# A modulation stream moved off TensorE's row products: VectorE, ScalarE and GpSimd accumulate, two-column products sum

## The chip, the cores and the metric

The kernel runs on one core of one Trainium2 chip. The metric is the device time of one execution in microseconds. A core has TensorE (PE; its weight loads are shown as PEld), VectorE (DVE), ScalarE (ACT) and GpSimd (POOL), each with a queue that it works off in order, and a queue (SP) that issues the transfers from device memory.

## The reference, cut to what matters

Two sequences, of 256 and 512 tokens, go through two layers of width 1024. In each layer a vector `c` of the sequence gives six modulation vectors, which scale and shift the normed input of the mixer and of the feed-forward network and gate their outputs:

```python
def trunk(x, c, adaln_w, adaln_b, norm_g, ...):
    for l in range(DEPTH):
        mod = jax.nn.silu(c) @ adaln_w[l] + adaln_b[l]
        sh1, sc1, g1, sh2, sc2, g2 = [t[:, None, :] for t in jnp.split(mod, 6, axis=-1)]
        h = rmsnorm(x, norm_g[l, 0]) * (1 + sc1) + sh1
        y = mlstm_mixer(...) if l % N_MIXERS == 0 else swa_mixer(...)
        x = x + g1 * y
        h = rmsnorm(x, norm_g[l, 1]) * (1 + sc2) + sh2
        x = x + g2 * conv_ffn(...)
    return rmsnorm(x, final_g)
```

`adaln_w[l]` is 1024 x 6144 float32: 24 MB in each layer, read once, for two vectors only. The product is small in arithmetic and large in bytes. The first mixer is an mLSTM with four heads, run forwards and backwards; the second is windowed attention.

## The kernel before, in words

All 768 tokens of both sequences are worked on together. Activations lie transposed, 128 channels on the partitions and tokens along the free axis. Products that need float32 accuracy are made of three products: each operand is split into a rounded part and a remainder (`fp_copy_split`: ScalarE writes the rounded `whi`, L236; VectorE subtracts it from the source to get `wlo`, L237), and TensorE adds high x high, high x low and low x high (L230 is the line of its helper `mm`).

Weights and modulation rows come through one set of staging buffers, `raw`, of five slots of 128x1024 (L245 issues the transfer). SP issues them in order; an issue that waits for a free slot holds up all those behind it.

The modulation is worked off beside the first mixer. `adaln_w[l]` is cut into six groups of 1024 columns, and each group into eight rows of 128x1024 (a "row" below is one such 128x1024 block). Groups 0 and 1 of layer 0 are needed at once and are done in the opening (`vector`); the change does not touch them. The rest was done in two streams, written as generators, of which the mixer takes a step at fixed places in its own code:

- `fillp`: groups 2 to 5 of layer 0 (`adaln_g`). For each row TensorE makes four products with `silc` (silu(c), two used columns in 32) as the stationary operand, one in each quarter of its columns, and accumulates over eight rows in one PSUM bank `ps`. At the end of a group the sums, which lie along the free axis, are copied to `sb` (a tile in a `raw` slot; VectorE and ScalarE, half each) and turned into columns by two transposes.
- `fill`: all six groups of layer 1 (`adaln_v`). For each row VectorE makes two operations, one for each sequence: `acc[:, s] = row * silc[:, k, s] + acc[:, s]` (L472; for the first row of a group a plain scaling, L470). The accumulator `ada` has one buffer. At the end of a group TensorE sums over the partitions by four products with 32 columns of ones, `sb` takes the result, and four transposes make columns.

In both, VectorE then adds the bias and writes `mod[l]`, and for groups 1 and 4 the `gain`.

Steps are taken: in the heads' query and key projections (`gemmT`, after each evacuation, and once after each half), in the value projection (`gemmN`, `values`, on every second token tile from `fill`, on the others from `fillp`), twice ahead of each sequence in a head's second part, and after each of the 16 products of the output gate. Counted from the code, the mixer offers 50 steps to `fill`, which has 49 to give, and 37 to `fillp`, which has 36.

Other work that the prediction's steps touch: the scores' weights are built by ScalarE as `E` and split into `PT`; each head's output `hs` is divided by `dn`, its mean square `ss` goes through a power on GpSimd (L942), and TensorE transposes it (L949). GpSimd also adds the masks `kct` (L829) and multiplies the gate `sg` (L966). The norms sum squares over partitions by products with `inv`, a 128x2 moving operand, the squares being the stationary one.

The order on each engine is written by a planner that plays the program through with its own costs, except in the opening, where TensorE, ScalarE and VectorE follow the order of the code.

Of the kernel before, what the change touches and what calls it, by code (L numbers as in the profile page):

```python
# [46 lines left out]
NG = 0  # L47
AB = NG + 32
# [97 lines left out]
class Net:  # L146
# [260 lines left out]
                )  # L407
        yield

    def adaln_g(self, l, grp):  # L410

        nc = self.nc
        fetch = lambda k: self.raw(
            self.io["adaln_w"][l, k * P : (k + 1) * P, grp * 1024 : (grp + 1) * 1024]
        )
        part = fetch(0)
        yield
        ps = self.ps()
        for k in range(KC):
            cur = part  # L420
            if k < KC - 1:
                part = fetch(k + 1)
            for g in range(4):
                r0 = 32 * g
                self.mm(
                    ps[r0 : r0 + 32, :256], self.silc[:, k, :], cur[:, g * 256 : (g + 1) * 256], k == 0, k == KC - 1
                )
            if k < KC - 1:
                yield
        sb = self.stg.tile([P, 2, P], F32, tag="raw", name=self.nm("sb"), bufs=5)  # L430
        nc.vector.tensor_copy(sb[:, 0], ps[:, :P])
        nc.scalar.copy(sb[:, 1], ps[:, P : 2 * P])
        pt = self.ps()[:, : 2 * P]
        for b in range(2):
            nc.tensor.transpose(pt[:, b * P : (b + 1) * P], sb[:, b], self.ident)
        src = pt.rearrange("p (b g s) -> p g b s", b=2, g=4)
        dst = self.mod[l][:, grp * 8 : (grp + 1) * 8, :].rearrange("p (g b) s -> p g b s", g=4)
        ab = self.cst(AB + 48 * l + 8 * grp, 8).rearrange("p (g b) -> p g b", g=4)
        for s in range(2):
            nc.vector.tensor_tensor(dst[:, :, :, s], src[:, :, :, s], ab, ALU.add)  # L440
        i = {1: 0, 4: 1}.get(grp)
        if i is not None:
            for s in range(2):
                nc.vector.scalar_tensor_tensor(
                    self.gain[l][i][:, :, s], self.mod[l][:, grp * 8 : (grp + 1) * 8, s], 1.0,
                    self.cst(NG + (2 * l + i) * 8, 8), ALU.add, ALU.mult,
                )
        yield

    def adaln_v(self, l, pool):  # L450

        nc = self.nc
        stt = nc.vector.scalar_tensor_tensor
        rows = [(grp, k) for grp in range(6) for k in range(KC)]
        fetch = lambda grp, k: self.raw(
            self.io["adaln_w"][l, k * P : (k + 1) * P, grp * 1024 : (grp + 1) * 1024]
        )
        raw = fetch(*rows[0])
        yield
        for grp, k in rows:  # L460
# [3 lines left out]
            if (grp, k) != rows[-1]:  # L464
                raw = fetch(*rows[grp * KC + k + 1])
            for s in range(2):
                w = self.silc[:, k, s : s + 1]
                if k == 0:
                    with self.tc.issue_after(self.behind_gates.ins):
                        nc.vector.tensor_scalar(acc[:, s], row, w, None, ALU.mult)  # L470
                else:
                    stt(acc[:, s], row, w, acc[:, s], ALU.mult, ALU.add)  # L472
            if k < KC - 1:
                yield
                continue
            ps = self.ps()
            for s in range(2):
                for b in range(2):
                    r0 = 32 * (2 * s + b)
                    self.mm(ps[r0 : r0 + 32, :], self.ones[:, :32], acc[:, s, b * 512 : (b + 1) * 512], True, True)  # L480
            sb = self.stg.tile([P, 2, 256], F32, tag="raw", name=self.nm("sb"), bufs=5)
            sb = [sb[:, z] for z in range(2)]
            nc.vector.tensor_copy(sb[0], ps[:, :256])
            nc.scalar.copy(sb[1], ps[:, 256:])
            pt = self.ps()
            for t in range(4):
                nc.tensor.transpose(
                    pt[:, t * P : (t + 1) * P], sb[t // 2][:, (t % 2) * P : (t % 2 + 1) * P], self.ident
                )
            src = pt.rearrange("p (t g s) -> p g t s", t=4, g=4)[:, :, :, 0]  # L490
            ab = self.cst(AB + 48 * l + 8 * grp, 8).rearrange("p (b t) -> p b t", b=2)
            dst = self.mod[l][:, grp * 8 : (grp + 1) * 8, :].rearrange("p (b t) s -> p b t s", b=2)
            for s in range(2):
                nc.vector.tensor_tensor(dst[:, :, :, s], src[:, 2 * s : 2 * s + 2], ab, ALU.add)
            i = {1: 0, 4: 1}.get(grp)
            if i is not None:
                for s in range(2):
                    stt(
                        self.gain[l][i][:, :, s], self.mod[l][:, grp * 8 : (grp + 1) * 8, s], 1.0,
                        self.cst(NG + (2 * l + i) * 8, 8), ALU.add, ALU.mult,  # L500
                    )
            yield


    def modulated(self, l, i):
# [260 lines left out]
    def mlstm(self, pool, xt, rows, raws):  # L766
        nc, io = self.nc, self.io
# [6 lines left out]
        F, a, M, z = (B[0:G, j] for j in range(4))  # L774
# [12 lines left out]
        with self.tc.manual_schedule(engines={eng.PE, eng.Activation, eng.DVE}):  # L787
# [14 lines left out]
            for s0, s1 in SEQS:  # L802
                b = slice(s0, s1)
# [18 lines left out]
        for h in range(4):  # L822
# [13 lines left out]
            for i in range(2 if h else 0):  # L836
                t = self.slab([P, 2, 2, T], R)
                for c, w in self.halves(U_MIN + 3 * h + i):
                    for q in (0, 1):
                        keep(t, i, c)(q, self.gemmT(w, q))  # L840
                        if q <= c or h > 1:
                            self.step(self.fill)
                    self.step(self.fillp)
                qk.append(t)
            qt, kt = qk

            def values():
# [4 lines left out]
                def evac(t, o):  # L852
                    self.fp_copy_split(v[:, 0, t, :256], v[:, 1, t, :256], o)
                    if t % 2 == 0:
                        self.step(self.fill)
                    elif h:
                        self.step(self.fillp)

                self.gemmN(U_MIN + 3 * h + 2, evac)
                return v  # L860
# [49 lines left out]
            ss = pool.tile([P, T6], F32, tag="ss", name=self.nm("ss"), bufs=2)  # L910
            for q, (s0, s1) in enumerate(SEQS):
                n = (s1 - s0) // P
                self.step(self.fillp, 2)
                hq = []
                for i in range(n):
                    ti = s0 // P + i
# [688 lines left out]
    def first(self, pool):  # L1605
# [11 lines left out]
        def chain(*gens):  # L1617
            for g in gens:
                yield from g
# [4 lines left out]
        for _ in chain(self.fillp, self.fill):  # L1624
            pass
        return act

# [128 lines left out]
```

## Time and profile before

| | us |
|---|---|
| median of 3 runs | 1871.75 (1870.81 to 1874.26) |
| the profiled execution: its time | 1875.08 |
| its span, first to last instruction | 1873.0 |
| TensorE busy in the span | 1801.3 (96%) |
| VectorE | 1400.9 (75%) |
| ScalarE | 911.0 (49%) |
| GpSimd | 497.9 (27%) |
| granted TensorE clock, mean | 0.988 |

"Busy" is the time in which at least one instruction of the engine ran; TensorE's instructions overlap, so the distance between two starts says more of their price than their own durations. Rows of the timeline give start, duration, engine, line, operation, tile written <- tiles read, shapes and count; in brackets stands the idle time before and what ended it. Rows of one tile give shortest, median and longest duration in ns. Rows of groups give count, busy time in us, mean ns, and the idle time before them.

### The profile page before, as it was taken

How to read it: one execution, taken by the hardware profiler on the slowest of the kernel's cores; microseconds unless marked ns; L12 is line 12 of the kernel's file. 1: busy time of each engine (PE TensorE's matmuls, PEld its weight loads, DVE VectorE, ACT ScalarE, POOL GpSimd, SP SyncE). 2: the span in 40 equal slices, each digit the busy share in tenths (PEclk: the TensorE clock that was granted, in tenths of full speed). 3: DMA queues.
4: the chain of work that ended last, by engine and by line, in shares of the span. 5: the costliest groups of instructions: out<-in, count | busy, mean ns of one | idle time of the engine just before them, and what ended most of it. 6: DMA issues, size and time to landing. Idle time of an engine off the chain costs nothing. (4 is left out here: it accounts for less than half of the span.)

```text
span 1873.0 us, 29153 instructions
## 1 busy us (share of the span) xinstructions
PE 1801.3 (96%) x11306; PEld 1662.3 (89%) x11306; DVE 1400.9 (75%) x2306; ACT 911.0 (49%) x1841; POOL 497.9 (27%) x390
## 2 busy tenths in 40 slices
PE   6989999999999999999999999989999999999997
PEld 5968887878988999999999898879989999999996
DVE  4866567685689777777777768875997777777777
ACT  4544334444455444444444556763565444444443
POOL 2011001031024333333331313330134333333322
PEclk9999999999999999999999999999999999999999
DMA  8353466555212222222222221212222222222211
GB/s 325 108 165 134 152 197 205 162 167 193 97 50 74 68 68 68 68 68 68 68 68 82 101 90 41 89 55 90 79 79 79 68 68 68 68 68 68 68 35 68
DMA packets 64246, 184.49 MB, mean 99 GB/s; under 512 B 6167, under 2 KB 23831, under 8 KB 64108
## 3 DMA queue, kind: packets, MB, share of 16 engines
q1 hardware_dynamic: 64108, 182.63, 30.1%
q8 instruction: 89, 1.46, 0.3%
q14 instruction: 49, 0.40, 0.1%
HBM read 176.17 MB, written 6.43 MB: 97 GB/s over the span
## 5 line engine op out<-in xcount | busy, mean ns | idle before, releaser
L236 ACT CAST whi<-raw 128x1024 fp32r<-128x1024 f32 x237 | 249.0, 1051 | 389.9 <-PE pa L230 198.6
L237 DVE TENSOR_TENSOR wlo<-raw,whi 128x1024 fp32r<-128x1024 f32 x237 | 316.3, 1335 | 108.8 <-ACT whi L236 107.7
L230 PE MATMUL pa<-slab,whi 128*128 128x256 f32 (+1 forms) x1472 | 346.9, 333 | 6.2 <-DVE slab L719 6.2
L230 PEld LDWEIGHTS pa<-slab,whi 128*128 128x128 f32 x1472 | 253.2, 190 | 33.1 <-DVE slab L719 7.1
L719 DVE SCALAR_TENSOR_TENSOR slab<-pa,mod,slab 128x256 f32<-128x256 f32 (+1 forms) x368 | 207.5, 591 | 70.9 <-PE pa L230 70.6
L230 PE MATMUL ps<-zh,whi 128*128 128x256 f32 (+2 forms) x688 | 233.4, 340 | 6.3 <-ACT whi L236 2.6
L230 PE MATMUL pa<-slab,wlo 128*128 128x256 f32 (+1 forms) x736 | 234.9, 331 | 0.0
L230 PE MATMUL ps<-zh,wlo 128*128 128x256 f32 (+2 forms) x688 | 228.3, 334 | 3.8 <-DVE wlo L237 3.8
L230 PE MATMUL ps<-zl,whi 128*128 128x256 f32 (+2 forms) x688 | 228.7, 334 | 1.4 <-DVE zl L539 0.9
L1275 PE MATMUL ps<-zh,whi 128*128 128x384 f32 x504 | 171.0, 339 | 6.4 <-ACT ps L1330 5.4
L1276 PE MATMUL ps<-zl,whi 128*128 128x384 f32 x504 | 169.7, 337 | 0.8 <-DVE zl L1233 0.8
L1277 PE MATMUL ps<-zh,wlo 128*128 128x384 f32 x504 | 169.0, 335 | 0.0
L230 PEld LDWEIGHTS pa<-slab,wlo 128*128 128x128 f32 x736 | 139.3, 190 | 12.9 <-DVE wlo L237 0.9
L230 PEld LDWEIGHTS ps<-zh,whi 128*128 128x128 f32 x688 | 132.2, 192 | 20.3 <-issue 3.5
L230 PEld LDWEIGHTS ps<-zh,wlo 128*128 128x128 f32 x688 | 132.2, 192 | 14.6 <-DVE wlo L237 4.6
L230 PEld LDWEIGHTS ps<-zl,whi 128*128 128x128 f32 x688 | 132.3, 192 | 10.7 <-DVE zl L539 1.1
L1531 POOL TENSOR_TENSOR slab<-slab 128x772 f32<-128x772 f32 x44 | 87.4, 1987 | 190.3 <-DVE slab L1503 178.9
L1306 POOL TENSOR_TENSOR raw<-raw,raw 128x512 f32<-128x512 f32 x40 | 53.7, 1341 | 291.7 <-DVE wlo L237 243.8
L1502 DVE SCALAR_TENSOR_TENSOR slab<-slab,cstt,slab 128x771 f32<-128x771 f32 x88 | 106.2, 1208 | 25.4 <-ACT slab L1500 25.4
L1503 DVE SCALAR_TENSOR_TENSOR slab<-slab,cstt,slab 128x771 f32<-128x771 f32 x88 | 120.1, 1365 | 0.8
L1303 POOL TENSOR_TENSOR raw<-raw 128x512 f32<-128x512 f32 x40 | 64.8, 1619 | 186.1 <-DMA raw<-in_w_dram 178.4
L472 DVE SCALAR_TENSOR_TENSOR ada<-raw,silc,ada 128x1024 f32<-128x1024 f32 x84 | 111.5, 1358 | 2.6 <-DMA raw<-in_adaln_w_dram 2.6
(300 smaller groups left out, 4163.8 us busy)
## 6 DMA issues: line engine op xcount, KB each, us to landing
raw<-in_w_dram SPq DMA_DIRECT2D x208, 512.0 KB, 3.7
raw<-in_adaln_w_dram SPq DMA_DIRECT2D x84, 512.0 KB, 4.5
slab<-in_x_dram SPq DMA_DIRECT2D x12, 512.0 KB, 7.7
slab<-in_adaln_w_dram SPq DMA_DIRECT2D x12, 512.0 KB, 10.3
slab<-mrows SPq DMA_DIRECT2D x8, 384.0 KB, 6.0
xs<-slab SPq DMA_DIRECT2D x6, 512.0 KB, 2.9
bt<-brow SPq DMA_DIRECT2D x16, 192.0 KB, 3.2
slab<-xs SPq DMA_DIRECT2D x6, 512.0 KB, 5.7
```

Source lines behind the costliest of these rows:

```text
L230: self.last_mm = self.nc.tensor.matmul(out, lhsT, rhs, start=start, stop=stop)
L236: nc.scalar.copy(hi, src)
L237: return nc.vector.tensor_tensor(lo, src, hi.bitcast(F32), ALU.subtract)
L472: stt(acc[:, s], row, w, acc[:, s], ALU.mult, ALU.add)
L719: self.nc.vector.scalar_tensor_tensor(x, o, self.mod[l][:, gc + c, q : q + 1], x, ALU.mult, ALU.add)
L1275: mm(o, wh[:, k], hi[k], start=start and k == 0, stop=False, skip_group_check=True)
L1276: mm(o, wh[:, k], lo[k], start=False, stop=False, skip_group_check=True)
L1277: mm(o, wl[:, k], hi[k], start=False, stop=k == 3, skip_group_check=True)
L1303: tt(q[2], q[2], q[3], ALU.add)
L1502: stt(y[:, 1:], u[:, :-1], w(0), y[:, 1:], ALU.mult, ALU.add)
L1503: stt(y[:, :-1], u[:, 1:], w(2), y[:, :-1], ALU.mult, ALU.add)
L1531: nc.gpsimd.tensor_tensor(y, y, yrow[:, j], ALU.mult)
```

## The change

The two streams become one, `later`: layer 0's groups 2 to 5, then all of layer 1's, 80 rows in order. A row's first sequence is still accumulated by one operation of VectorE. For the second, ScalarE scales the row in place, and GpSimd adds it to the accumulator. For the first row of a group ScalarE writes the accumulator directly. At the end of a group each 128x128 block of the accumulator is the stationary operand of a product with two columns of ones, 16 products in all, which leave the sums as columns in PSUM; `sb` and the transposes are gone. All the places that took a step of `fillp` take one of `fill`; 87 steps are offered, and 81 are to be given.

```diff
-    def adaln_g(self, l, grp):
...
-    def adaln_v(self, l, pool):
+    def later(self, pool):
         nc = self.nc
+        rows = [(l, grp, k) for l, grps in ((0, range(2, 6)), (1, range(6))) for grp in grps for k in range(KC)]
...
+        for n, (l, grp, k) in enumerate(rows):
             if k == 0:
                 acc = pool.tile([P, 2, 1024], F32, tag="ada", name=self.nm("ada"), bufs=1)
             row = raw
+            if n + 1 < len(rows):
+                raw = fetch(*rows[n + 1])
+            with self.tc.issue_after(self.behind_gates.ins) if n == 0 else ExitStack():
+                self.rows_in(acc, row, k)
             if k < KC - 1:
                 yield
                 continue
-            ps = self.ps()
+            pm = self.ps()[:, : 4 * KC]
             for s in range(2):
-                for b in range(2):
-                    r0 = 32 * (2 * s + b)
-                    self.mm(ps[r0 : r0 + 32, :], self.ones[:, :32], acc[:, s, b * 512 : (b + 1) * 512], True, True)
...
+                for b in range(KC):
+                    i = 2 * (s * KC + b)
+                    self.mm(pm[:, i : i + 2], acc[:, s, b * P : (b + 1) * P], self.ones[:, 0:2], True, True)
+            src = pm.rearrange("p (s b z) -> p s b z", s=2, z=2)
...
+    def rows_in(self, acc, row, k):
+        nc = self.nc
+        w = [self.silc[:, k, s : s + 1] for s in range(2)]
+        if k == 0:
+            nc.vector.tensor_scalar(acc[:, 0], row, w[0], None, ALU.mult)
+            nc.scalar.activation(acc[:, 1], row, AF.Copy, scale=w[1])
+            return
+        nc.vector.scalar_tensor_tensor(acc[:, 0], row, w[0], acc[:, 0], ALU.mult, ALU.add)
+        nc.scalar.activation(row, row, AF.Copy, scale=w[1])
+        nc.gpsimd.tensor_tensor(acc[:, 1], acc[:, 1], row, ALU.add)
...
-                    self.step(self.fillp)
+                    self.step(self.fill)
...
-        self.fillp = chain(*(self.adaln_g(0, grp) for grp in range(2, 6)))
-        self.fill = self.adaln_v(1, pool)
+        self.fill = self.later(pool)
```

More of the change, by code (lines that the diff above doesn't have):

```diff
@@ L408, in vector @@
         yield
-    def adaln_g(self, l, grp):
+    def later(self, pool):
         nc = self.nc
[L413 to L417, printed above, removed]
-        ps = self.ps()
[L419 to L433, printed above, removed]
-        for b in range(2):
[L435 to L448, printed above, removed]
-    def adaln_v(self, l, pool):
[L452 to L455, printed above, removed]
+        rows = [(l, grp, k) for l, grps in ((0, range(2, 6)), (1, range(6))) for grp in grps for k in range(KC)]
+        fetch = lambda l, grp, k: self.raw(
             self.io["adaln_w"][l, k * P : (k + 1) * P, grp * 1024 : (grp + 1) * 1024]
@@ L475, in adaln_v @@
                 continue
-            ps = self.ps()
+            pm = self.ps()[:, : 4 * KC]
             for s in range(2):
-                for b in range(2):
-                    r0 = 32 * (2 * s + b)
-                    self.mm(ps[r0 : r0 + 32, :], self.ones[:, :32], acc[:, s, b * 512 : (b + 1) * 512], True, True)
[L481 to L492, printed above, removed]
+                for b in range(KC):
+                    i = 2 * (s * KC + b)
+                    self.mm(pm[:, i : i + 2], acc[:, s, b * P : (b + 1) * P], self.ones[:, 0:2], True, True)
+            src = pm.rearrange("p (s b z) -> p s b z", s=2, z=2)
+            ab = self.cst(AB + 48 * l + 8 * grp, 8)
             for s in range(2):
-                nc.vector.tensor_tensor(dst[:, :, :, s], src[:, 2 * s : 2 * s + 2], ab, ALU.add)
+                dst = self.mod[l][:, grp * 8 : (grp + 1) * 8, s]
+                nc.vector.tensor_tensor(dst, src[:, s, :, 0], ab, ALU.add)
             i = {1: 0, 4: 1}.get(grp)
@@ L912, in mlstm @@
                 n = (s1 - s0) // P
-                self.step(self.fillp, 2)
+                self.step(self.fill, 2)
                 hq = []
```

19 lines of the change are left out of this document (3 added, 16 removed).

## The prediction

> **What bounds the kernel now.** I read the page first, then the stretch of the first mixer in windows, then what TensorE waits for there, then single rows for prices.
>
> The page: TensorE is busy nearly throughout, VectorE three quarters of the time, GpSimd little.
>
> ```profile
> span 1873.0 us, 29153 instructions
> PE 1801.3 (96%) x11306; PEld 1662.3 (89%) x11306; DVE 1400.9 (75%) x2306; ACT 911.0 (49%) x1841; POOL 497.9 (27%) x390
> ```
>
> The change touches only the stretch from 85 to 446 us, where the modulation rows are worked in. In windows (length, busy time of each engine, granted clock, DMA), with the waits of TensorE in that stretch (total, times, longest):
>
> ```profile
> 85.00:365.00 280.00, 267.54 (x1902) 228.53 (x1901) 184.14 (x333) 114.16 (x310) 21.85 (x14) 0.99 0.52 168
> 365.00:446.00 81.00, 77.00 (x438) 65.33 (x438) 63.57 (x78) 31.26 (x64) 22.96 (x18) 0.96 0.51 163
> ...
> PE pa L949 <- ACT hs L945: 5.8, 2, 5.4
> PE ps L230 <- DVE wlo L237: 3.8, 4, 1.7
> PE ps L230 <- ACT whi L236: 2.6, 2, 1.4
> PE pa L230 <- ACT hs L936: 1.5, 1, 1.5
> PE ps L487 <- ACT sb L484: 0.9, 1, 0.9
> PE ps L487 <- DVE sb L483: 0.6, 1, 0.6
> ```
>
> TensorE works 344.5 of 361 us, so the stretch is TensorE's work plus some 16 us of waits. VectorE is at 247.7 us (69%), ScalarE at 145.4, GpSimd at 44.8. The change pays only through TensorE work or those waits; a saved VectorE microsecond alone is worth nothing.
>
> **TensorE work removed.** Layer 0's groups 2 to 5 lose 32 row products (four 32-column products each, eight records), layer 1 loses 24 products with ones, and both lose 24+8 transposes. Busy time of each in the stretch (TensorE first), and two places that show start-to-start prices:
>
> ```profile
> 85.00:446.00 361.00, 19.54 (x256) 6.94 (x256) 120.41 (x96) 0.00 (x0) 0.98 0.52 167
> 85.00:446.00 361.00, 7.43 (x48) 1.07 (x48) 0.00 (x0) 0.00 (x0) 0.98 0.52 167
> ...
> 293.77 0.66 PE L487 MATMUL ps<-kct,sb 128*128 128x128 f32 x4 [0.95 <-ACT sb L484]
> 294.26 0.38 PE L949 MATMUL pa<-kct,hs 128*128 128x128 f32 x2
> ```
>
> Row products 19.5 us (first row, tile silc), ones products 7.4 (second, tile ones). Four transposes last 294.26−293.77 = 0.49 us, so 32 are 3.9. Together 30.9 us. The two waits for sb (0.9+0.6) go as well, since sb is gone: 1.5. But one piece saves nothing:
>
> ```profile
> 126.05 1.50 PE L230 MATMUL ps<-raw,silc 128*32 128x256 f32 x24
> 129.03 3.86 PE L230 MATMUL pa<-slab,PT 128*128 128x258 f32 x30 [1.47 <-ACT hs L936]
> 138.29 0.69 PE L949 MATMUL pa<-kct,hs 128*128 128x128 f32 x2 [5.40 <-ACT hs L945]
> ```
>
> These three row products stand in front of waits for hs of 1.47 and 5.40 us; without them TensorE waits 1.5 us longer for the same hs. The two 1.5s cancel.
>
> **TensorE work added.** Ten groups of 16 products, stationary 128x128 f32, moving two columns. The norm sums are the same form, two records per product (nine products, 18 records):
>
> ```profile
> 483.97 2.06 PE L230 MATMUL pa<-inv,nt 128*128 128x2 f32 x18
> 485.89 0.60 PE L230 MATMUL ps<-slab,whi 128*128 128x384 f32 x2
> ```
>
> Start to start 485.89−483.97 = 1.92 us for 18 records, 0.107 each. 160 products are 320 records: 34.1 us. Two columns do not make a product cheap; loading its weights twice sets the price. So TensorE's work does not shrink: 34.1 − 30.9 = **+3.2 us**.
>
> **VectorE, ScalarE, GpSimd.** Rows for the prices (ns min/median/max; then xcount, busy us and mean ns):
>
> ```profile
> L472 DVE SCALAR_TENSOR_TENSOR ada<-raw,silc,ada x84: 1267/1276/2869, 87.6 to 427.8; 128x1024 f32<-128x1024 f32 x84
> L470 DVE TENSOR_SCALAR ada<-raw,silc x12: 744/748/1207, 85.4 to 401.0; 128x1024 f32<-128x1024 f32 x12
> L236 ACT CAST whi<-raw 128x1024 fp32r<-128x1024 f32 x28 | 29.3, 1046 | 44.2 <-DMA raw<-in_w_dram 44.2
> L1306 POOL TENSOR_TENSOR raw<-raw,raw x40: 1288/1297/2016, 520.9 to 1800.8; 128x512 f32<-128x512 f32 x40
> L1531 POOL TENSOR_TENSOR slab<-slab x44: 1842/1867/2838, 565.4 to 1830.4; 128x772 f32<-128x772 f32 x44
> ```
>
> VectorE: 84 accumulations and 12 scalings (120.4 us) become 70 x 1.27 + 10 x 0.74 = 96.3; the ten sb copies go with them. ScalarE: 80 scalings at about 1.05 us (the cast of the same 128x1024), +84 us, to 229 of 361. GpSimd: 70 adds of 128x1024. 512 columns take 1.288, 772 take 1.842, so 2.13 ns a column and an estimated 2.38 us each: +167 us, to 212 of 361. By averages all three fit. But VectorE and GpSimd do not run freely side by side:
>
> ```profile
> L1503 DVE SCALAR_TENSOR_TENSOR slab<-slab,cstt,slab x88: 1004/1022/2587, 561.4 to 1829.2; 128x771 f32<-128x771 f32 x88
> L1315 POOL TENSOR_TENSOR raw<-raw,raw x40: 1284/2012/2205, 557.5 to 1803.5; 128x512 f32<-128x512 f32 x40
> ...
> 302.42 1.31 DVE L444 SCALAR_TENSOR_TENSOR gain<-mod,cstt 128x8 f32<-128x8 f32 x2
> 303.80 4.06 DVE L472 SCALAR_TENSOR_TENSOR ada<-raw,silc,ada 128x1024 f32<-128x1024 f32 x2
> 308.24 1.21 DVE L237 TENSOR_TENSOR wlo<-raw,whi 128x1024 fp32r<-128x1024 f32 x1
> ...
> 301.77 3.82 POOL L829 TENSOR_TENSOR slab<-slab,kct 128x768 f32<-128x768 f32 x2 [8.62 <-DMA slab<-mrows]
> ...
> 309.50 0.50 PE L230 MATMUL ps<-zh,wlo 128*128 128x512 f32 x1 [1.72 <-DVE wlo L237]
> ```
>
> An operation of VectorE with two SBUF inputs takes up to 2.6 times its shortest, and GpSimd's add 2.0 instead of 1.28. The five lines after that are the whole case in small: GpSimd adds masks from 301.77 to 305.59; meanwhile two 8-column gains take 1.31 us and two row accumulations 4.06 instead of 2.5; the weight remainder wlo starts at 308.24; TensorE waits 1.72 us for it. The change puts 70 such adds, each longer than these, into the same stretch.
>
> The Trainium skill (SBUF — State Buffer, Terms) says that VectorE and GpSimd share a port pair that is locked for a whole instruction, so that the loser blocks fully; the trace agrees in kind, with the 2869 ns accumulation above against 1267. By that rule in full the sum below would be some +28 us, by the rows as I read them +11.
>
> **Waits.** (a) Weight splits. GpSimd will be at work 212/361 = 59% of the time; a blocked VectorE operation loses on average half an add, 1.2 us, so about 0.7 us per two-input operation. Those that count are splits finished just in time: six TensorE waits for wlo or whi above. A wlo has at least one other operation ahead of it, so some 1.4 us each, 8.4 (a cast behind one of ScalarE's scalings, 1.05 us, is within that); against it, a row now holds VectorE for 1.27 us instead of two in a row (2.47). I take +5; bounds −6 (all six waits gone) and +20 (27 remainders in this stretch, 0.7 each). (b) Ends of groups. TensorE's products now wait for the last add on GpSimd, behind ScalarE: 1.05+2.38 = 3.4 us after the row landed, where VectorE took 2.5, plus blocking. Behind a waiting product stands all TensorE work, its queue being in order; behind the products the next group's first scaling on VectorE and ScalarE, since the accumulator has one buffer. The planner will place most products late enough: +3 for ten groups; bounds 0 and 15 (1.5 each). (c) GpSimd's queue. The power for ss (L942), the product with sg (L966) and the masks (L829) now stand behind row adds, up to 2.4 us each; TensorE has other heads' products to do except at 133–138 us. In (b)'s bound. (d) SP's queue. The row transfers are 80 as before, in one stream; a row's staging slot is now freed by GpSimd, later than by TensorE or VectorE, but the ten sb tiles leave those five slots, and one prefetched row instead of two sits in them. Taken as +0, bounds −3 and +5. (e) The clock. After long waits it is halved:
>
> ```profile
> 137.00:143.00 6.00, 4.71 (x21) 4.37 (x22) 1.31 (x4) 3.44 (x10) 4.26 (x3) 0.50 0.00 2
> 407.00:413.00 6.00, 5.70 (x13) 4.47 (x14) 6.00 (x9) 1.05 (x1) 0.00 (x0) 0.50 0.78 257
> ```
>
> Both follow waits (5.40 us before 138.29, the waits for splits before 407), and each costs half of at least 6 us, so 3 or a little more. With half as much waiting again I add one: +3; bounds −3 and +9.
>
> **Sum.** 3.2 + 5 + 3 + 3 = +14, less 3 because one accumulating PSUM bank is no longer held across eight steps and TensorE gets it back: **+11 us**. The profiled execution took 1875.08 us, 1873.0 of it span; against it the sum is 1886. It ran 3.3 over the median 1871.75, so for medians I say **1883**.
>
> **Rivals.** *Faster: the transfers win.* The splits are late because weights land late: ScalarE waited 44.2 us for them (row of L236 above), SP waiting for staging slots:
>
> ```profile
> SPq L245 <- PE ps L230: 71.2, 16, 15.3
> SPq L245 <- DVE ada L472: 56.1, 23, 4.1
> ```
>
> One stream with fewer slots taken would bring weights earlier; then the waits for wlo and whi (6.4), the half-clock after 407 (3) and the bank's 3 go, against +3.2 of work: −9, about 1863. It decides if weights land over 2.4 us earlier than now, which covers one add. Against it: rows keep their slots through GpSimd.
>
> *Same.* The planner hides splits and groups, and the work's +3.2 meets 3 from the bank: 1872.
>
> *Port bound.* If GpSimd and VectorE's SBUF work excluded each other throughout, their times would add:
>
> ```profile
> L237 DVE TENSOR_TENSOR wlo<-raw,whi 128x1024 fp32r<-128x1024 f32 x27 | 34.0, 1259 | 17.1 <-ACT whi L236 17.1
> L237 DVE TENSOR_TENSOR PT<-E,PT 128x640 fp32r<-128x640 f32 x16 | 13.0, 820 | 0.2
> L237 DVE TENSOR_TENSOR slab<-sg,slab 128x512 fp32r<-128x512 f32 x8 | 5.5, 684 | 6.3 <-ACT slab L236 6.3
> ```
>
> Rows 96, these 52, GpSimd 212: 360 us in a stretch of 361. Fully packed it would just fit; with a tenth of the time lost between dependent steps it needs 400, +39. I take some two thirds of that, as the rows show blocking that is strong and not total: +28, 1900.
>
> *The slot rival.* GpSimd lags in bursts and holds staging slots, so weights come later still: a step in the value products comes every 24 products of 0.12 us, 2.9 us,
>
> ```profile
> 272.44 0.28 PE L230 MATMUL ps<-wlo,zh 128*128 128x256 f32 x1
> 272.56 0.28 PE L230 MATMUL ps<-whi,zh 128*128 128x256 f32 x1
> ```
>
> and an add blocked for half a microsecond more than its 2.38 takes as long. As (d)'s and (a)'s upper ends, 3.2+20+5, also near 1900.
>
> **Chances.** Moderate slowdown 0.45 (1876 to 1892), port bound 0.10, slots 0.05, same 0.17, faster 0.23. Less than 0.2% (3.7 us) cannot be told from no change. The moderate case and the last two slow rivals make slower 0.60. The range leaves out a tenth at each end: 1863 to 1902; the likeliest case's own is 1876 to 1892.
>
> **What would show it.** After: TensorE records of the two-column products start 0.107 us apart, 320 of them, about 34 us; TensorE's busy time in the stretch not lower. GpSimd adds of 128x1024 near 2.4 us at their shortest and over 3 on average; row accumulations averaging above 1.358 us (mean now); more and longer waits for wlo; products waiting for the add. Wrong if adds and accumulations keep their shortest times together, if the waits for wlo and whi shrink, or if products cost less than 0.2 us each.

## The result and the profile after

The changed kernel takes 1935.47 us (median of 4 runs, 1934.1 to 1937.23) against 1872.26 us before (1870.81 to 1874.26): a ratio of 1.0338 [1.0324, 1.0352], 63 us slower. The direction was predicted, the size was not: 1883 was forecast, and 1935 lies far above the range's end of 1902.

The first lines of the page after: span, then busy time, share and instructions of each engine.

```profile
span 1935.3 us, 29388 instructions
PE 1829.7 (95%) x11290; PEld 1706.6 (88%) x11290; DVE 1488.4 (77%) x2280; ACT 990.1 (51%) x1911; POOL 703.9 (36%) x460
```

By averages nothing is full except TensorE, as before. The span grew by 62.3 us. The stretch in which the modulation is worked in begins at 85 us in both kernels; measured to the first product of the out projection it grew from 360.9 to 424.5 us, 63.6 more, so the whole loss lies there. The stretch in a window of its own (length, busy time of TensorE, its weight loads, VectorE, ScalarE and GpSimd, granted clock, DMA):

```profile
85.00:509.00 424.00, 374.14 (x2312) 340.37 (x2310) 331.73 (x383) 225.02 (x443) 252.24 (x101) 0.90 0.46 146
```

Before, this row read 344.54, 293.86, 247.71, 145.43 and 44.81 us at a clock of 0.98 in 361 us. VectorE does less work now and is busy 84 us longer: that is the first sign that its operations wait inside themselves. The groups of the stretch show where (count, busy us, mean ns, idle before):

```profile
L457 DVE SCALAR_TENSOR_TENSOR ada<-raw,silc,ada 128x1024 f32<-128x1024 f32 x70 | 149.0, 2129 | 1.0 <-DVE dn L891 0.3
L237 DVE TENSOR_TENSOR wlo<-raw,whi 128x1024 fp32r<-128x1024 f32 x28 | 51.5, 1838 | 25.9 <-ACT whi L236 25.9
L891 DVE TENSOR_TENSOR dn<-dn,eT 128x2 f32<-128x2 f32 x24 | 16.7, 699 | 7.9 <-ACT dn L888 7.9
L237 DVE TENSOR_TENSOR slab<-ps,slab 128x256 fp32r<-128x256 f32 x30 | 12.2, 413 | 2.2 <-ACT slab L236 2.2
L459 POOL TENSOR_TENSOR ada<-ada,raw 128x1024 f32<-128x1024 f32 x70 | 202.6, 2894 | 178.0 <-ACT raw L458 155.3 <-ACT dn L888 19.5
```

Three of these groups before:

```profile
L472 DVE SCALAR_TENSOR_TENSOR ada<-raw,silc,ada 128x1024 f32<-128x1024 f32 x84 | 111.5, 1358 | 2.6 <-DMA raw<-in_adaln_w_dram 2.6
L237 DVE TENSOR_TENSOR slab<-ps,slab 128x256 fp32r<-128x256 f32 x30 | 12.4, 418 | 19.0 <-ACT slab L236 18.8
L934 DVE TENSOR_TENSOR dn<-dn,eT 128x2 f32<-128x2 f32 x24 | 5.0, 213 | 19.2 <-ACT dn L931 19.2
```

The accumulations average 2129 ns (1358 before), the weight remainders `wlo` 1838 (1259). Even `dn`, two columns wide, went from 213 to 699 ns. The fourth row of the table after is the control: a split with one of its two inputs in PSUM, 418 ns before and 413 now. The same holds for every operation of VectorE with an input in PSUM: none changed its mean by more than 10 ns. Those that lose have their inputs in SBUF, nearly all of them two inputs; the exceptions are the eight operations on `ss`, two and four columns wide, which name one tile and went from 166 to 1409 and 1214 ns. The scalings of rows (L454), whose second input is a column, did not lose: 747 ns now. The same seen in time, sixteen microseconds of VectorE and then of GpSimd (start, duration; in brackets the idle time before):

```profile
300.60 3.10 DVE L457 SCALAR_TENSOR_TENSOR ada<-raw,silc,ada 128x1024 f32<-128x1024 f32 x1
303.62 0.41 DVE L237 TENSOR_TENSOR slab<-ps,slab 128x256 fp32r<-128x256 f32 x1
303.95 3.05 DVE L457 SCALAR_TENSOR_TENSOR ada<-raw,silc,ada 128x1024 f32<-128x1024 f32 x1
306.93 0.41 DVE L237 TENSOR_TENSOR slab<-ps,slab 128x256 fp32r<-128x256 f32 x1
307.26 3.08 DVE L457 SCALAR_TENSOR_TENSOR ada<-raw,silc,ada 128x1024 f32<-128x1024 f32 x1
...
311.86 0.72 DVE L891 TENSOR_TENSOR dn<-dn,eT 128x2 f32<-128x2 f32 x1 [1.19 <-ACT dn L888]
...
312.80 3.29 DVE L237 TENSOR_TENSOR wlo<-raw,whi 128x1024 fp32r<-128x1024 f32 x1
...
299.33 15.68 POOL L459 TENSOR_TENSOR ada<-ada,raw 128x1024 f32<-128x1024 f32 x5
```

GpSimd's five adds run without a gap at 15.68/5 = 3.14 us each, where their shortest is 2.34; VectorE's accumulations take some 3.1 where their shortest is 1.27. One add beside one accumulation would take 2.34 + 1.27 = 3.61 if they excluded each other; the step measured is 3.35 (303.95 − 300.60). The split of TensorE's results, which is what TensorE's next product needs, is short itself but waits behind 3 us of accumulation. What TensorE waits for (total, times, longest):

```profile
PE pa L906 <- ACT hs L902: 8.6, 3, 5.9
PE pa L230 <- ACT hs L893: 8.5, 1, 8.5
PE ps L230 <- DVE slab L240: 8.5, 2, 6.4
PE ps L230 <- DVE wlo L237: 6.2, 3, 2.9
PE pa L230 <- DVE slab L910: 3.9, 3, 1.9
PE pa L230 <- DVE E L850: 3.3, 3, 2.0
```

Before, the list was headed by 5.8 us for `hs`; the waits for `wlo` and `whi`, 6.4 us together, are 6.2 now. What grew are the waits for work further down the queues of VectorE and ScalarE. ScalarE is held up too: its scaling in place has to wait until VectorE has read the row, and behind the scaling stand the operations on `hs`:

```profile
ACT raw L458 <- DVE ada L457: 69.5, 40, 6.2
```

And behind the waits the clock is halved for long times, for example

```profile
144.00:158.00 14.00, 7.29 (x21) 5.93 (x22) 12.79 (x17) 6.79 (x18) 13.84 (x6) 0.50 0.66 226
```

In the stretch TensorE stands idle 50.3 us (16.5 before), and the granted clock is at half for 85.3 us (13.7 before). Idle time gives 33.8 of the 63.6 us. The other 29.8 are longer working time, of which 3.2 is the added work by the prediction's prices. The remaining 26.6 fit the clock: TensorE was busy in 68.0 us of the half-clock time (11.5 before), and half of the 56.5 added is 28.

### The profile page after: what moved, and what is told of

Read it like the earlier page. It is cut to its first block, busy times and chain, and to the rows that moved or that the text cites. A ratio compares the mean times of both kernels' runs of the same rounds, so it can differ in the third digit from the quotient of the medians.

```text
span 1935.3 us, 29388 instructions
## 1 busy us (share of the span) xinstructions
PE 1829.7 (95%) x11290; PEld 1706.6 (88%) x11290; DVE 1488.4 (77%) x2280; ACT 990.1 (51%) x1911; POOL 703.9 (36%) x460
## 4 chain that ended last, share of the span: by engine, by line
PE 69%; DVE 17%; issue 5%; ACT 5%; POOL 2%; DMA 2%; SPq 0%; POOLq 0%; DVEq 0%; ACTq 0%
PE pa L230 20%; PE ps L230 19%; PE ps L1232 10%; PE ps L1233 9%; PE ps L1234 9%; DVE ada L457 4%; DVE wlo L237 2%; DMA raw<-in_w_dram 1%; PE pa L1073 1%; ACT whi L236 1%; POOL ada L459 1%; DVE slab L237 1%; DVE PT L237 1%; DVE slab L676 1%; DVE slab L1460 1%
## 5 line engine op out<-in xcount | busy, mean ns | idle before, releaser
L237 DVE TENSOR_TENSOR wlo<-raw,whi 128x1024 fp32r<-128x1024 f32 x237 | 334.4, 1411 | 115.2 <-ACT whi L236 114.2
L459 POOL TENSOR_TENSOR ada<-ada,raw 128x1024 f32<-128x1024 f32 x70 | 202.6, 2894 | 178.0 <-ACT raw L458 155.3
L1263 POOL TENSOR_TENSOR raw<-raw,raw 128x512 f32<-128x512 f32 x40 | 53.4, 1335 | 291.3 <-DVE wlo L237 244.1
L457 DVE SCALAR_TENSOR_TENSOR ada<-raw,silc,ada 128x1024 f32<-128x1024 f32 x70 | 149.0, 2129 | 1.0 <-DVE dn L891 0.3
L458 ACT ACTIVATE raw<-raw,silc 128x1024 f32<-128x1024 f32 x70 | 80.5, 1151 | 100.5 <-DVE ada L457 69.5
## 6 DMA issues: line engine op xcount, KB each, us to landing
slab<-in_adaln_w_dram SPq DMA_DIRECT2D x12, 512.0 KB, 10.2
```

The lines of the kernel that those rows point to most:

```text
L237: return nc.vector.tensor_tensor(lo, src, hi.bitcast(F32), ALU.subtract)
L457: nc.vector.scalar_tensor_tensor(acc[:, 0], row, w[0], acc[:, 0], ALU.mult, ALU.add)
L458: nc.scalar.activation(row, row, AF.Copy, scale=w[1])
L459: nc.gpsimd.tensor_tensor(acc[:, 1], acc[:, 1], row, ALU.add)
```

## The experiments

**What is compared.** Three theories. *Port*: the two-input operations of VectorE on SBUF and GpSimd's operations exclude each other, and their sum fills the stretch. *Slots*: GpSimd frees the rows' staging slots late, and SP, which waits for it 194.9 us in all, brings weights late:

```profile
SPq L245 <- POOL ada L459: 194.9, 55, 8.5
```

*Ending*: the two-column products wait for GpSimd's last add, or cost the clock. For each run its time stands below, and where the argument needs them the stretch's length, TensorE's idle time, the half-clock time and the **port time**. The port time is worked out thus: each VectorE operation with two SBUF inputs and each GpSimd operation of the stretch counts with the shortest duration of its form (5th percentile over these runs), and all are added (the scalings of rows are counted too, 7 to 15 us, though they do not lose). Before it is 180.1 + 36.6 = 216.7 us, 60% of the stretch; after, 161.6 + 201.9 = 363.5, or 85.6%.

**e1, without the add.** The second sequence's sums are left out.

```diff
-        nc.gpsimd.tensor_tensor(acc[:, 1], acc[:, 1], row, ALU.add)
```

> The changed kernel without GpSimd's 70 adds; ScalarE still scales each row in place. It leaves out the second sequence's sums beyond each group's first row. Port theory (GpSimd's adds and VectorE's two-input operations lock each other out): GpSimd in the stretch falls to about 45 us, the row accumulations of VectorE fall from a mean of 2129 ns to under 1400, the time to 1870 to 1882 (before plus the 3 us of TensorE work). Rival, waits for the add (TensorE's products and the staging slots wait for GpSimd): the same 1870 to 1882, so this run does not tell the two apart. Rival, TensorE (the 160 two-column products and the order they are put in): stays above 1920.

1885.66 us, ratio 1.0071 [1.0056, 1.0086]. The stretch falls to 374.6 us, idle to 9.5, port time to 199.1 (53%). So the adds are worth 49.8 of the 63 us, and some 15 remain without them; the time lies 4 us above what both theories expected, which the endings below account for.

**e2, the adds apart.** As many GpSimd operations of nearly the same size, which read and write only a tile of their own and free the slot early. The second sequence is left out.

```diff
-        nc.gpsimd.tensor_tensor(acc[:, 1], acc[:, 1], row, ALU.add)
+        self.apart(self.addpool, row)
...
+    def apart(self, pool, row):
+        tok = pool.tile([P, 2], F32, tag="tok", name=self.nm("tok"), bufs=4)
+        self.nc.scalar.copy(tok, row[:, 0:2])
+        self.nc.gpsimd.tensor_tensor(self.side[:, 0:2], self.side[:, 0:2], tok, ALU.add)
+        self.nc.gpsimd.tensor_tensor(self.side, self.side, self.side, ALU.mult)
```

> The changed kernel, but GpSimd's 70 operations work on a tile of their own (992 columns, two inputs, paced by a two-column copy that ScalarE takes of each row): no product waits for them, and ScalarE frees the row's slot. It leaves out the second sequence's sums. Port theory: VectorE is locked out as before, row accumulations still average 1900 ns or more, the time stays at 1915 or more. Waits theory: nobody waits for GpSimd, so 1870 to 1885. TensorE theory: above 1920.

1904.2 us, 1.0177 [1.0159, 1.0194]; stretch 390.8, idle 28.5, half clock 47.8 us. Operations whose results nobody waits for cost 18.5 us over e1, where the adds cost 49.8. Both expectations missed: the time lies between them, and the accumulations average 1635 ns, not 1900. This looked like a large share for the slots or the products. But the operation was also cheaper (1836 ns at its shortest against 2338 in the changed kernel, rows below at e15 and e16), and the port time lower (342.2, 87.6%): two causes were changed at once, which e15 to e17 separate.

**e7, the same side operations beside the old streams.** Base is the kernel before. VectorE has as many operations as there, but sums both sequences of layer 1 into one half of the accumulator, so layer 1's modulation is not complete.

```diff
+            if k:
+                self.apart(self.addpool, cur)
...
-                    stt(acc[:, s], row, w, acc[:, s], ALU.mult, ALU.add)
+                    stt(acc[:, 0], row, w, acc[:, 0], ALU.mult, ALU.add)
+            if k:
+                self.apart(pool, row)
```

> The kernel before, with 70 two-input operations of GpSimd on a tile of their own (992 columns), one beside each row but a group's first, paced by a two-column copy of the row that ScalarE takes; nothing waits for them. Its layer-1 sums of the two sequences go into one accumulator, with the same operations of VectorE, so that half of the modulation of layer 1 is left out. Port theory: row accumulations slow from 1358 ns to 1900 or more, and the time rises by 35 to 65 us, to 1907 to 1937. Waits theory and TensorE theory: 1872 to 1880 (the ScalarE copies are 0.2 us each).

1912.1 us, 1.022 [1.0204, 1.0236]. With the old row products and endings, and no result of GpSimd used, the loss is 41 us, as the port theory expected. Port time 354.9 in 400.4 us, 88.6%. The accumulations are slow here too, 1779 ns on average (shortest, median, longest):

```profile
L474 DVE SCALAR_TENSOR_TENSOR ada<-raw,silc,ada x84: 1264/1285/2928, 89.4 to 475.5; 128x1024 f32<-128x1024 f32 x84
```

**e15 and e16, the slot freed early.** The GpSimd operation works on the accumulator's second half and does not read the row; ScalarE's two-column copy frees the slot. The second sequence is left out in both. In e15 both inputs are the accumulator and are multiplied, in e16 the second is another tile and is added:

```diff
-        nc.gpsimd.tensor_tensor(acc[:, 1], acc[:, 1], row, ALU.add)
+        self.apart(self.addpool, row, acc)
...
+        tok = pool.tile([P, 2], F32, tag="tok", name=self.nm("tok"), bufs=2)
+        self.nc.scalar.copy(tok, row[:, 0:2])
+        self.nc.gpsimd.tensor_tensor(acc[:, 1, 0:2], acc[:, 1, 0:2], tok, ALU.add)
# e15
+        self.nc.gpsimd.tensor_tensor(acc[:, 1], acc[:, 1], acc[:, 1], ALU.mult)
# e16
+        half = acc[:, 1].rearrange("p (b c) -> p b c", b=KC)
+        self.nc.gpsimd.tensor_tensor(half, half, self.ident.unsqueeze(1).to_broadcast([P, KC, P]), ALU.add)
```

> The changed kernel with GpSimd's 70 operations on the accumulator alone (1024 columns, two inputs, paced by a two-column copy of the row that ScalarE takes), so that ScalarE frees the row's staging slot; the products still wait for GpSimd. The second sequence's sums are left out. Slot theory (most of the 31 us between the changed kernel and the adds on a tile of their own come from slots held until GpSimd is done): 1900 to 1912. Waiting-products theory (they come from TensorE waiting for the last add and the next group waiting for TensorE): 1922 or more.

> As the run that freed the slot, but GpSimd adds a 128x128 constant, repeated eight times, to the accumulator, so that the operation has two different inputs and costs its full 2.34 us, as in the changed kernel (there it cost 1.89); ScalarE frees the row's slot, products wait. The second sequence's sums are left out. Slot theory: 1905 to 1918, clearly under the changed kernel's 1935. Port theory (it was the cheaper operation, not the slot, that saved 24 us): 1925 or more.

e15: 1911.67 us, 1.0214 [1.0197, 1.0231]; e16: 1937.92 us, 1.0352 [1.0329, 1.0376]. e15 alone would have spoken for the slots, 24 us saved. The rows of the GpSimd operation (of e2, e15, e16, then of the changed kernel; shortest, median and longest ns) show why it does not:

```profile
L470 POOL TENSOR_TENSOR side<-side x70: 1836/1841/2890, 96.3 to 436.9; 128x992 f32<-128x992 f32 x70
L468 POOL TENSOR_TENSOR ada<-ada x70: 1890/1897/2983, 95.6 to 458.6; 128x1024 f32<-128x1024 f32 x70
L469 POOL TENSOR_TENSOR ada<-ada,kct x70: 2347/2408/3457, 95.0 to 485.2; 128x1024 f32<-128x1024 f32 x70
L459 POOL TENSOR_TENSOR ada<-ada,raw x70: 2338/3092/3463, 88.3 to 470.9; 128x1024 f32<-128x1024 f32 x70
```

With the same columns as both inputs the operation takes 1.89 us, with two different inputs 2.35 like the add in the changed kernel (2.34). That e15 multiplies and e16 adds is not the reason: among GpSimd's operations of 128x512 with two different inputs, the product with `sg` takes 1264 ns at its shortest and the differences (L1263, L1264) 1270 and 1292. With the full-priced operation and the slots freed early, the kernel is as slow as the changed one. 70 x 0.457 = 32 us of port time gave 26 us of time.

So the slots do not carry the loss, however long SP waits. That they cost nothing is not shown: e16 also has 70 two-column operations of GpSimd that the changed kernel lacks, 14 us of port time by their shortest duration (0.2 us each). If these cost their full price, freed slots gained about as much and the two hide each other; that leaves the slots some 16 us of the 63 at most (14/0.86, the share being worked out below).

**e17, the products free of GpSimd.** The add goes into a tile that no product reads; the row is still read and the slot still held. The second sequence is left out.

```diff
-        nc.gpsimd.tensor_tensor(acc[:, 1], acc[:, 1], row, ALU.add)
+        nc.gpsimd.tensor_tensor(self.side, self.side, row, ALU.add)
```

> The changed kernel with GpSimd adding each scaled row to a tile of its own, at full price: the row's slot is held until the add is done, but no product and no next group waits for it. The second sequence's sums are left out. Slot theory: 1925 or more. Waiting-products theory: 1912 or less.

1945.05 us, 1.0382 [1.036, 1.0404]: not faster, but 10 us slower than the changed kernel, for which no run gives the reason. Products that wait for the last add do not carry the loss either; slots and port this run does not part, since the slot is still held. The changed kernel's wait of that kind was 0.2 us in all.

**The port's share.** The seven kernels with 70 GpSimd operations of 992 or 1024 columns are the changed one, e2, e5 (below), e7, e15, e16 and e17. Their port time is 85.6, 87.6, 83.3, 88.6, 86.5, 88.7 and 84.4% of the stretch, at lengths from 390.8 to 438.4 us and whatever is done with the results. None of the seven others (before, e1, e3, e4, e10, e11, e20) exceeds 78%. In these seven kernels the stretch is about port time/0.86, within some 3%. The four that free the slots early have the higher shares, 86.5 to 88.7 against 83.3 to 85.6; without their two-column operations they have 83 to 86% like the others, so this too leaves open whether the slots or the price of those operations makes the difference.

**e5, e10, e4: the endings.** e5 is the changed kernel with the old ending (ones products, `sb`, four transposes) in all ten groups; e10 is e5 without the add (second sequence left out); e4 is the kernel before with the two-column products in layer 1's six groups. The edit, as in e5 and e10 (e4 has it the other way round):

```diff
-                for b in range(KC):
-                    i = 2 * (s * KC + b)
-                    self.mm(pm[:, i : i + 2], acc[:, s, b * P : (b + 1) * P], self.ones[:, 0:2], True, True)
+                for b in range(2):
+                    r0 = 32 * (2 * s + b)
+                    self.mm(ps[r0 : r0 + 32, :], self.ones[:, :32], acc[:, s, b * 512 : (b + 1) * 512], True, True)
+            sb = self.stg.tile([P, 2, 256], F32, tag="raw", name=self.nm("sb"), bufs=5)
...
+                nc.tensor.transpose(
```

> The changed kernel with the old ending of a group (four products with ones, sb, four transposes) in place of the 16 two-column products, all ten groups. Clock theory: half-clock time in the stretch falls from 85 us by 30 or more, and TensorE has 16 us less to do, but the port and the waits for GpSimd stay: 1895 to 1912. Port theory alone: TensorE is not the bound, so 1920 or more.

> The changed kernel without GpSimd's adds (so without the second sequence's sums beyond a group's first row) and with the old ending. Clock theory: half-clock time falls from 55 us to 20 or less and TensorE's work by 16 us, so 1852 to 1865, under the kernel before. Price theory: 16 us less than the run without adds, 1868 to 1874.

> The kernel before, with one part of the change alone: the sums of layer 1 (six groups) become columns by two-column products, no sb, no transposes. Clock theory (a full burst of 32 two-column records, 3.5 us, makes the clock gate halve the clock, as it did behind every unbroken burst of the run without adds): +10 us of TensorE work, and 3.4 to 6.8 us at half clock behind most of the six bursts, so half-clock time in the stretch rises from 14 us to 40 or more, another +10 to +17: 1890 to 1900. Price theory (the products cost their 0.107 us a record and nothing else): 1878 to 1884, half-clock time under 25.

e5: 1953.97 us, 1.0441 [1.0426, 1.0457]; e10: 1865.09 us, 0.9965 [0.9954, 0.9977]; e4: 1882.21 us, 1.006 [1.0044, 1.0076]. Without the adds the old ending is 20.6 us better (e1 to e10); with them it is 18.5 us worse (changed to e5). In e4 six groups cost 10.9 us against the runs beside it (1871.3); their added TensorE work by the prediction's prices is 6 x 32 x 0.107 − 7.4 − 24 x 0.49/4 = 10.2. So e4 came out as its price theory expected, although its half-clock time rose to 30.7 us (13.7 before); e10 lies at the upper end of what its clock theory expected. Ten groups would be some 17, and e1 to e10 shows 20.6. In the stretch, e1 has 31.6 us more of TensorE's busy time than e10 and 9.7 less idle time. What the 31.6 hold beyond the prices, some 15 us, goes with the clock: half-clock time is 54.6 us in e1 and 13.7 in e10, though TensorE stands idle longer in e10 (19.2 us against 9.5). Windows of e1 around one group's products, and the records in them:

```profile
258.00:261.00 3.00, 3.00 (x27) 3.00 (x27) 2.54 (x9) 2.30 (x9) 0.00 (x0) 1.00 0.00 0
261.00:264.40 3.40, 3.40 (x33) 3.40 (x33) 0.76 (x2) 0.68 (x2) 0.00 (x0) 1.00 0.00 0
264.90:268.10 3.20, 3.20 (x17) 3.20 (x17) 3.13 (x4) 2.10 (x2) 0.00 (x0) 0.50 0.36 87
268.30:272.00 3.70, 3.70 (x33) 3.70 (x33) 2.89 (x3) 2.46 (x3) 0.00 (x0) 1.00 0.70 208
...
261.05 3.63 PE L230 MATMUL ps<-ones,ada 128*128 128x2 f32 x32
```

TensorE counts as busy throughout, and yet the clock is halved for one period right behind 32 two-column records in a row. In e1 a half-clock period begins in or right behind each of the seven bursts of 30 or 32 in a row (one of these also stands behind a wait of 2.4 us); in e4 behind the products of five of its six groups, while one burst of 32 in a row has none.

For e5, 1920 or more was expected from the port alone, and so it came; that it is slower than the changed kernel was not expected. Why the old ending loses with the adds is read, not tested: e5's port time of 365.2 us is that of the changed kernel, but its stretch is 438.4 us (83.3%) and TensorE's idle time 78.4, and its waits name the longer chain, in which VectorE must copy `sb` behind blocked accumulations:

```profile
PE ps L230 <- DVE wlo L237: 10.9, 5, 3.6
PE pa L230 <- ACT slab L236: 11.0, 6, 3.1
PE ps L441 <- DVE sb L437: 6.4, 5, 3.5
```

The waits for `sb` are new, but 6.4 us are not 18.5; the reason for the rest stays open.

**e3 and e11, both sequences on VectorE.** One stream without GpSimd and without ScalarE's scaling, complete; e3 with the new ending, e11 with the old.

```diff
-        nc.scalar.activation(row, row, AF.Copy, scale=w[1])
-        nc.gpsimd.tensor_tensor(acc[:, 1], acc[:, 1], row, ALU.add)
+        nc.vector.scalar_tensor_tensor(acc[:, 1], row, w[1], acc[:, 1], ALU.mult, ALU.add)
```

> The changed kernel with both sequences of a row accumulated by VectorE, and neither ScalarE nor GpSimd in the stream: 140 accumulations at 1.27 us and 20 scalings at 0.74 are 193 us where VectorE had 120 before, so VectorE is at about 320 of 361 us, its own bound nearly. Port theory: accumulations average under 1400 ns; 1876 to 1892, some 45 us better than the changed kernel although VectorE has 97 us more to do. Waits theory: the same range. TensorE theory: above 1920.

> One stream, both sequences on VectorE, neither ScalarE nor GpSimd in it, and the old ending of a group. TensorE as the bound: 16 us under the same with two-column products (1903), 1883 to 1890. VectorE as the bound (about 330 of 361 us, and the old ending puts two more copies and a longer chain behind it, as it did behind GpSimd's adds): 1900 or more.

e3: 1903.0 us, 1.0161 [1.0144, 1.0178]; e11: 1898.67 us, 1.0142 [1.0117, 1.0167]. Both beat the changed kernel by over 30 us with the same outputs, because little is blocked (accumulations 1319 and 1323 ns on average). Both are slower than before, e3 11 us above its expected range and e11 just under what it expected of VectorE as the bound. Windows of e3, then e11, show VectorE busy 80 and 83% of the stretch. That TensorE's operands now wait behind it is read from this, not tested; e3 also pays for its ending.

```profile
85.00:474.00 389.00, 363.43 (x2327) 332.82 (x2325) 312.75 (x467) 145.51 (x365) 45.62 (x31) 0.93 0.51 159
85.00:468.00 383.00, 343.74 (x2125) 297.89 (x2123) 316.66 (x476) 147.90 (x374) 52.97 (x31) 0.94 0.52 161
```

**e20, the sums along the free axis.** If TensorE's ending and the port both cost, a better version has neither. Base is the kernel before; layer 1's matrix is handed over transposed, in 48 blocks of 128 output channels x 1024, and one VectorE operation for each block and sequence multiplies by silu(c), repeated on all partitions, and sums along the row, straight into the column of `mod`. No accumulator, ones products, `sb` or transposes are left for layer 1.

```diff
-                    stt(acc[:, s], row, w, acc[:, s], ALU.mult, ALU.add)
+                ttr = lambda to, c0, c1, first: nc.vector.tensor_tensor_reduce(
+                    out=to, in0=row[:, c0:c1], in1=self.crep[:, s, c0:c1], op0=ALU.mult, op1=ALU.add, scale=1.0,
+                    scalar=first, accum_out=out,
+                )
...
+                    if s:
+                        ttr(row, 0, D, bias)
+                    else:
+                        side = self.ps()
+                        ttr(side, 0, 512, bias)
+                        ttr(side, 512, D, out)
...
-                nc.tensor.transpose(
```

> The kernel before, with layer 1's modulation weights stored with the outputs on the partitions, so that VectorE's multiply-and-reduce gives a column at once: no accumulator, no products with ones, no sb, no transposes. TensorE has 11 us less to do and loses the 1.5 us of waits for sb; VectorE does 48 x (one reduction of 1024 and two of 512, about 2.8 us) = 134 us instead of 120. If TensorE's work and waits are the bound of the kernel before: 1858 to 1866. If VectorE's 14 us more delay the weight splits: 1868 to 1878.

1863.88 us (1860.77 to 1865.56), 0.9954 [0.9934, 0.9974]: faster than both kernels, by 0.5% against the one before, as expected, and complete. Its window and the operation's rows:

```profile
85.00:431.00 346.00, 330.70 (x2256) 286.74 (x2255) 269.10 (x583) 144.79 (x368) 50.21 (x31) 0.99 0.55 173
L465 DVE CUSTOM_DVE_ANT_0 raw<-raw,crep,cstt x48: 1266/1280/2955, 87.0 to 427.6; 128x1024 f32<-128x1024 f32 x48
L465 DVE CUSTOM_DVE_ANT_0 ps<-raw,crep,cstt x48: 743/754/2373, 84.3 to 424.9; 128x512 f32<-128x512 f32 x48
```

TensorE is busy 13.8 us less than before in the stretch (330.70 against 344.54), VectorE 21 more, and with GpSimd at 50 us VectorE has the port mostly for itself.

## Why the prediction was wrong

The mechanism was named, the size was not. The step that failed is the weighing of the **port bound**: its sum of 360 us was near (the port time measured is 363.5, though VectorE's part, 148, was 14 too low and GpSimd's, 212, 10 too high, and the two cancel). Its tenth lost between dependent steps, which would make 400 us, was itself too little: the stretch took 424.5, so a seventh was lost. But the prediction then took "some two thirds" of that, +28, gave it a chance of 0.10 because blocking looked "strong and not total", and based the forecast on average blocking of 0.7 us for those operations that finish just in time. The overlap is where it failed, and the runs show the blocking to be nearly total: in the whole trace of the changed kernel GpSimd's operations and VectorE's with two SBUF inputs are in flight together for 412 us and run 353 us over their shortest durations (5th percentile of each form), 86% of it, and the kernel before had already much the same share, 214 of 257 us, 83%. What was in doubt, the kind of the lock, could have been worked out from the trace of before. The share of 0.86 could not: it is read from the seven kernels themselves, the changed one among them, and why a seventh of the stretch is lost stays open.

The Trainium skill (SBUF — State Buffer, Terms) says that the loser of the shared port pair blocks fully, for the whole instruction. The trace agrees: accumulations of up to 3472 ns where the shortest is 1268 (row below), and 413 ns as before where one input is PSUM. The prediction's "by that rule in full +28" was not the rule in full, since it had kept the two thirds.

By its other steps:

- *TensorE work +3.2*: right in its prices. The 320 records are there,

```profile
L230 PE MATMUL ps<-ones,ada x320: 165/251/374, 119.6 to 481.2; 128*128 128x2 f32 x160
L457 DVE SCALAR_TENSOR_TENSOR ada<-raw,silc,ada x70: 1268/1286/3472, 85.8 to 460.9; 128x1024 f32<-128x1024 f32 x70
```

  and e4 paid 10.9 us where their prices gave 10.2. The clock behind the bursts was missing.
- *GpSimd 70 x 2.38*: right, 2338 ns shortest and 2894 on average; VectorE's 1.27 as well at its shortest, 1268 (second row).
- *(a) Weight splits +5, (b) ends of groups +3*: together with the gain of 3 they stand for TensorE's idle time, which grew by 33.8 us. The waits for `wlo` and `whi` did not grow in sum (6.2 us; before 6.4), where the prediction expected more; the idle time comes from everything that stands behind VectorE: `hs`, the splits of TensorE's results, E. The prediction counted operations that are blocked, not those queued behind them. (b) as named, a product waiting for an add, was 0.2 us; e17 agrees.
- *(c) GpSimd's queue* was put within (b)'s bound of 15. The largest waits now are for `hs`, one of 8.5 us; how much of that is GpSimd's queue no run separates.
- *(d) SP's queue, 0*: not contradicted. e16 frees the slots and is no faster, but up to some 16 us can hide there.
- *(e) The clock +3*: one period was added; half-clock time grew by 71.6 us, which costs up to 36. It follows both the waits and, as e1 and e10 show, the bursts of small products.
- *A bank returned, −3*: cannot be seen beside the rest.

Of the rivals, the faster one asked for weights 2.4 us earlier, and in e16 slots freed earlier made nothing faster than the changed kernel. The slot rival's condition came true, adds of 2.89 us on average where it named 2.9 for a step, but by e16 the slots can account for some 16 us of the 63 at most, not for the loss.

## What to carry to other kernels

Before work goes to GpSimd, add up the shortest durations of its operations and of VectorE's two-SBUF-input operations in that stretch; in this stretch it was the bound once the sum came near 85%, however empty both looked on the page. A wait by a busy queue (SP's 195 us) or an operation named in a chain is no cause until it is taken away by itself, at the same price of the operation: e15 and e16 differ in one operation's inputs and say opposite things. And a sum over partitions for few columns is cheaper not made at all: lay out the matrix, ahead of the launch, so that the sum runs along the free axis.

## What the runs showed of the hardware

By these traces, bursts of products with two moving columns count as rest for the clock. TensorE's 32 records take some 3.5 us without a gap at full clock, and a period of half clock mostly follows (3.41 us or a multiple): 54.6 us in e1 against 13.7 in e10, where only the ending differs. Within one run the half-clock periods all begin on one grid of 3.41 us. In the step of the grid ahead of eight of e1's ten periods TensorE was never idle and spent 2.3 to 3.4 us on two-column records; ahead of the other two it was idle for 1.87 us, and for 1.11 us with 0.92 us of such records. Ahead of e10's three it was idle for 1.65 to 2.11 us. The Trainium skill (TensorE: Matmul & The Clock Gate, Part 1) gives half rate after an idle window of about 3.4 us, free-running. The length of the periods and the grid agree; the idle time ahead of them can be shorter than a whole window here, and the bursts of two-column records are not idle time at all: there the measurement decides.

The shared port holds up even a two-column operation: `dn` takes up to 1255 ns in e1, where its median is 158, and 699 on average beside the adds. A GpSimd operation of 128x1024 float32 costs 1.89 us with the same columns as both inputs (e15) and 2.34 to 2.35 with two different ones (the changed kernel, e16).
